# A two-layer encoder on TensorE: activation tiles laid out chunk by chunk as first part and rest with tokens of one parity together, and the attention branch's output projection in two sums

## The chip, the cores and the metric

The kernel runs on one core of a Trainium2 chip. The time is device microseconds of one execution, and a kernel's time is the median of its runs. The core has a matrix engine (PE, with PEld for its weight loads), a vector engine (DVE), an activation engine (ACT), GpSimd (POOL) and a queue of transfers (SP).

## The reference

One sequence of 256 tokens with 1024 channels goes through two layers; all is float32.

```python
def reference(x, w_in, w_pool, ..., norm_f):
    h = x
    for layer in range(DEPTH):
        h = h + _token_mixer(_rmsnorm(h, norm1[layer]), w_in[layer], ...)
        h = h + _conv_ffn(_rmsnorm(h, norm2[layer]), w_up[layer], ...)
    return _rmsnorm(h, norm_f)
```

`_token_mixer` multiplies the normed tokens with one wide matrix `w_in`. Its columns are: 1024 of a pooling branch (four groups, centred means over 2, 4, 8 and 16 tokens minus the token, then a 256x256 matrix per group and a scale), three times 1536 of queries, keys and values (12 heads of 128 in three groups: all keys within 64 tokens, every 4th, every 16th token; the groups are combined by their softmax denominators into 4 x 128 channels), and two times 1024 of gates. The result is `sigmoid(g_pool) * (pool_out @ w_a) + sigmoid(g_attn) * (attn_out @ w_b)`, multiplied by `w_o`. `_conv_ffn` multiplies by `w_up` (two halves of 2816 columns), puts a width-3 convolution over the tokens and a gelu on the first half, multiplies it with the second and by `w_down`.

## The kernel before

**Two parts.** A float32 operand is kept as two tiles of type fp32r: a first part (`xh`, `wh`), which is the operand cast, and a rest (`xl`, `wl`), which is the operand minus that cast. A product is three passes: first by first, first by rest, rest by first.

**Weights** (class `Weights`). A list of pieces, in the order of use, is written out at lines 235 to 282. A transfer of 1 MB (L117, three buffers) brings two pieces. For each, ACT casts the first part (L177) and DVE subtracts it (L178). `get` takes the next piece and has the split of up to three pieces ahead put into the engines' queues; split pieces have five buffers, and a buffer is free when the matmuls of its old piece are done.

**Activations.** `x2` is a tile `[P, 2, KD, S]`: for each channel of a chunk of 128, the first parts of all eight chunks, then the rests, with the 256 tokens in their order. Tokens live in rows by parity (token 2m + t in row m of half t), because the residual stream `h` is `[P, 2, D]`.

- `to_channels` (L432) transposes normed tokens on PE, 128 at a time, and casts and subtracts into `x2` (L454, L455), writing every second word.
- `proj` (L479) makes 128 output channels for all 256 tokens. Per chunk, L485 multiplies `wh` with 512 moving columns (the first parts and the rests of one chunk, 8 KB apart) into both halves of a PSUM tile, and L486 multiplies `wl` with the 256 first parts into the second half. `add_up` (L490) adds the halves: an ACT copy (L492) and a DVE add (L493).
- `row_mm` (L495) and `v_sum` (L562) have the activations as the stationary operand and 512 columns of weights as the moving one: three passes each, on the tokens of one parity, read as `t::2`, every second word. `residual_mm` (L501) calls `row_mm` for the products that are added to `h`; `v_sum` makes the values and the first four chunks of the MLP.
- `first_values` (L697) makes the first layer's values; its raw tile `[P, KD, 2, P]` keeps tokens of one parity together, and L729 reads them in one run.
- `chunk_mm` (L472) makes the three passes as three matmuls of 256 columns, for the pooling matrices (L475 to L477 into pool_ps) and for `w_b` (the same lines into b_ps, called at L1000).

**Order of a layer.** Values; pooling projections (L796); queries and keys (L946) with the steps of attention (`scores`, `turn`, `weigh`) between them; `w_a` (L971); gates of the pooling branch (L986); then twice four gates (L993) and four chunks of `w_b` (L1000 to L1007); `w_o` with the residual; the MLP, where `up` (L1065) makes one chunk (a projection for each half, convolution, gelu) and after two chunks two rows of `w_down` are added. The order of instructions on each engine is chosen by a scheduler from the program's order, but for the beginning, where it is fixed by hand. PSUM has two pools of four banks, `acc` and `mm`.

**The block of w_b.** Per output chunk: 4 x 3 matmuls into b_ps, a DVE multiply with the gate that reads PSUM (L1002), a DVE add of the pooling branch (L1005), an ACT cast (L1006) and a DVE subtraction (L1007).

Of the kernel before, what the change touches and what calls it, by code (L numbers as in the profile page):

```python
# [10 lines left out]
F32 = mybir.dt.float32  # L11
# [193 lines left out]
def encoder(ctx, tc, x, w_in, w_pool, pool_scale, w_a, w_b, w_o, norm1, norm2, w_up, conv_w,  # L205
# [226 lines left out]
    def to_channels(xh, xl, psum, g):  # L432

        tag = "acc" if psum is acc else "mm"

        def fin(t, r, xn):
            for n in range(4):
                cc = slice(n * 256, (n + 1) * 256)  # L440
                nc.vector.scalar_tensor_tensor(
                    out=xn[:, cc], in0=h[:, t, cc], scalar=r[:, 0:1], in1=g[:, cc],
                    op0=ALU.mult, op1=ALU.mult,
                )
            for n in range(2):
                pt = psum.tile([P, 4, P], F32, tag=tag, name="xt_ps")
                ks = slice(4 * n, 4 * n + 4)
                for k in range(4):
                    c0 = (4 * n + k) * P
                    nc.tensor.transpose(pt[:, k, :], xn[:, c0 : c0 + P], ident)  # L450
                oh = xh[:, ks, :].rearrange("p k (m t) -> p k t m", t=2)[:, :, t, :]
                ol = xl[:, ks, :].rearrange("p k (m t) -> p k t m", t=2)[:, :, t, :]
                last = [
                    nc.scalar.copy(out=oh, in_=pt),  # L454
                    nc.vector.tensor_sub(out=ol, in0=pt, in1=oh.bitcast(F32)),  # L455
                ]
                if n == 0:
                    yield
            if t == 1:
                W.queue_behind(last, 6)  # L460

        return fin
# [9 lines left out]
    def chunk_mm(ps, wh, wl, xh, xl, nk):  # L472

        for k in range(nk):
            nc.tensor.matmul(ps, wh(k), xh[:, k, :], start=(k == 0), stop=False)  # L475
            nc.tensor.matmul(ps, wh(k), xl[:, k, :], start=False, stop=False)  # L476
            nc.tensor.matmul(ps, wl(k), xh[:, k, :], start=False, stop=(k == nk - 1))  # L477

    def proj(x2, nk=8):  # L479


        i, (wh, wl) = W.get()
        ps = mmp.tile([P, 2, S], F32, tag="mm", name="proj_ps")
        for k in range(nk):
            nc.tensor.matmul(ps, wh[:, k, :], x2[:, :, k, :], start=(k == 0), stop=False)  # L485
# [15 lines left out]
    def residual_mm(parts, n, done, hold=4, fill=None):  # L501
# [60 lines left out]
    def v_sum(ps, xh, xl, t, n, piece):  # L562

        _, (wh, wl) = piece
        passes = [(xh, wh, 0), (xh, wl, 0), (xl, wh, 0), (xh, wh, 1), (xh, wl, 1), (xl, wh, 1)]
        for m, (a, w, j) in enumerate(passes):
            nc.tensor.matmul(  # L567
                ps, a[:, 2 * n + j, t::2], w[:, j, :], start=(n + m == 0), stop=(n == 3 and m == 5)
            )

    def channel_tiles():
        x2 = big.tile([P, 2, KD, S], F32R, tag="x", name="x2")
        return x2[:, 0], x2[:, 1], x2
# [123 lines left out]
    def first_values(rs, raw_x, fs, done, pe, keep_values):  # L697

        xuh, xul = raw_x
        xh, xl, x2 = channel_tiles()  # L700
# [5 lines left out]
        for k in range(0, KD, 2):  # L706
            f = fs[k // 4][:, k % 4 : k % 4 + 2]
            for j in range(2):
                nc.vector.scalar_tensor_tensor(
                    out=f[:, j], in0=f[:, j], scalar=gcol[:, k + j : k + j + 1], in1=rows,  # L710
                    op0=ALU.mult, op1=ALU.mult,
                )
            oh, ol = (
                a[:, k : k + 2, :].rearrange("p k (m t) -> p k t m", t=2) for a in (xh, xl)
            )
            nc.scalar.copy(out=oh, in_=f)
            nc.vector.tensor_sub(out=ol, in0=f, in1=oh.bitcast(F32))
# [19 lines left out]
    for l in range(DEPTH):  # L737
# [21 lines left out]
        if l == 0:  # L759
            with tc.manual_schedule():  # L760
                begun = begin_values_of_x()
            x2 = first_values(*begun, keep_values)
            xh, xl = x2[:, 0], x2[:, 1]
        else:
            for g in range(NG):
                held = begun[0] if g == 0 else [W.get() for _ in range(4)]
                for t in range(2):
                    if g + t == 0:
                        ps = begun[1]
                    else:  # L770
                        ps = v_tile()
                        for n in range(4):
                            v_sum(ps, xh, xl, t, n, held[n])
                    keep_values(t, g, ps)
                for i, _ in held:
                    W.free(i)
# [8 lines left out]
        plh = big.tile([P, KD, S], F32R, tag="ybig", name="plh")  # L785
        pll = big.tile([P, KD, S], F32R, tag="xn", name="pll")
        pooled = {}
        for gi in range(3, -1, -1):
# [31 lines left out]
            ph, pl = plh[:, 2 * gi : 2 * gi + 2, :], pll[:, 2 * gi : 2 * gi + 2, :]  # L820
# [3 lines left out]
        def pool_out(poh, pol):  # L824
            for j in range(2):
                i, (wh, wl) = W.get()
                for gg in range(2):
                    ph, pl = pooled[2 * j + gg]
                    for oc in range(2):
                        ps = mmp.tile([P, S], F32, tag="mm", name="pool_ps")  # L830
# [6 lines left out]
                        nc.scalar.activation(poh[:, c, :], ps, AF.Copy, scale=sc)  # L837
                        nc.vector.scalar_tensor_tensor(
                            out=pol[:, c, :], in0=ps, scalar=sc, in1=poh[:, c, :].bitcast(F32),
# [11 lines left out]
        at2 = big.tile([P, 2, HPG, S], F32R, tag="at2", name="at2")  # L851
        ath, atl = at2[:, 0], at2[:, 1]
# [51 lines left out]
        def weigh(hh):  # L904
# [13 lines left out]
            oh = ath[:, hh, :].rearrange("p (m t) -> p t m", t=2)  # L918
            ol = atl[:, hh, :].rearrange("p (m t) -> p t m", t=2)
# [14 lines left out]
        for m, c in enumerate(PAIRS):  # L934
            if m == 1:
                po2 = big.tile([P, 2, KD, S], F32R, tag="m2", name="po2")
                poh, pol = po2[:, 0], po2[:, 1]
                pool_parts = pool_out(poh, pol)
# [51 lines left out]
        m2 = big.tile([P, 2, KD, S], F32R, tag="m2", name="m2")  # L990
        mh, ml = m2[:, 0], m2[:, 1]
        for c4 in range(2):
            ths = [gate(4 * c4 + j) for j in range(4)]  # L993
            for j2 in range(2):
                i, (wh, wl) = W.get()
                for j in range(2):
                    c = 4 * c4 + 2 * j2 + j
                    ps = mmp.tile([P, S], F32, tag="mm", name="b_ps")
                    cc = slice(j * P, (j + 1) * P)
                    chunk_mm(ps, lambda k: wh[:, k, cc], lambda k: wl[:, k, cc], ath, atl, 4)  # L1000
                    m = sm.tile([P, S], F32, tag="u", name="m")
                    nc.vector.scalar_tensor_tensor(  # L1002
                        out=m, in0=ths[2 * j2 + j], scalar=1.0, in1=ps, op0=ALU.add, op1=ALU.mult
                    )
                    nc.vector.tensor_add(out=m, in0=m, in1=pa[:, c, :])  # L1005
                    nc.scalar.copy(out=mh[:, c, :], in_=m)  # L1006
                    nc.vector.tensor_sub(out=ml[:, c, :], in0=m, in1=mh[:, c, :].bitcast(F32))  # L1007
                W.free(i)

        xh, xl, x2 = channel_tiles()  # L1010
        norm = Norm(to_channels(xh, xl, acc, g2))
        entry = []

        def begin_mlp():
# [3 lines left out]
            for n in range(3):  # L1018
                v_sum(ps, xh, xl, 0, n, held[n])
            entry.extend((held, ps))  # L1020
            return lambda: v_sum(ps, xh, xl, 0, 3, held[3])

        run(residual_mm(lambda k: (mh[:, k, :], ml[:, k, :]), KD, norm.add, fill=begin_mlp))
# [6 lines left out]
                big.tile([P, n, S], F32R, tag=f"{tag}{j}", name=f"act{tag}{j}")  # L1030
# [24 lines left out]
        for n in range(4):  # L1055
            v_sum(ps, xh, xl, 1, n, held[n])
# [8 lines left out]
        def up(f):  # L1065
# [16 lines left out]
            g = sm.tile([P, S], F32, tag="p", bufs=3, name="g")  # L1082
            add_up(g, sums)
# [15 lines left out]
            ah, al = (x[n >= HPG][:, n - HPG * (n >= HPG), :] for x in (acth, actl))  # L1099
            nc.scalar.copy(out=ah, in_=y2)  # L1100
            nc.vector.tensor_sub(out=al, in0=y2, in1=ah.bitcast(F32))
# [5 lines left out]
        def begin_values():  # L1107

            ps, held = v_tile(), [W.get() for _ in range(4)]
            for n in range(3):  # L1110
                v_sum(ps, xh, xl, 0, n, held[n])
            begun.extend((held, ps))
            return lambda: v_sum(ps, xh, xl, 0, 3, held[3])
# [11 lines left out]
        if l + 1 < DEPTH:  # L1125
            xh, xl, x2 = channel_tiles()
            late["norm"] = Norm(to_channels(xh, xl, mmp, g1))
# [33 lines left out]
```

## Time and profile before

| | |
|---|---|
| median of 3 runs | 891.43 us (890.87 to 891.78) |
| the profiled execution | 890.68 us |
| its span, first to last instruction | 888.9 us |
| granted TensorE clock | 0.999 |
| DMA | 164.47 MB, mean 185 GB/s |
| projections, L485 and L486 | 40.4% and 20.4% of the chain that ended last |
| row_mm, L497 to L499 | 6.3% each |
| v_sum, L567 | 6.3% |
| w_b, L475 to L477 into b_ps | 0.9% each |

The page gives, engine by engine, the busy time; then the span in 40 slices; then the chain that ended last, followed back from the last instruction to what released it; then groups of equal instructions, as "line engine operation out<-in, shape, xcount | busy us, mean ns of one | idle us before". Matmuls are pipelined: one starts before the one ahead of it has ended, so a group's mean duration is longer than what it adds to the time. The chain and the timeline list starts in microseconds, and from these the step between two matmuls is found.

### The profile page before, as it was taken

What the parts mean: (1) busy time and instruction counts of PE and PEld (TensorE: products, weight loads), DVE (VectorE), ACT (ScalarE), POOL (GpSimd) and SP (SyncE); (2) the same over time, 40 slices, a digit from 0 to 9 for tenths busy, and PEclk for the clock granted to TensorE, in tenths of its full rate; (3) what the DMA queues carried; (4) which work ended last, traced back from release to release, by engine and by line L of the source; (5) the groups of instructions that cost most, each with busy time, mean ns of one, the idle gap of its engine ahead of it and who ended that gap; (6) DMA issues with size and microseconds to landing.
All of it is one profiled execution on the core that took longest, in us unless ns stands there. A gap on an engine that the chain in (4) does not pass through costs nothing.

```text
span 888.9 us, 12895 instructions
## 1 busy us (share of the span) xinstructions
PE 881.2 (99%) x4913; PEld 764.5 (86%) x4913; DVE 671.2 (76%) x1135; ACT 516.0 (58%) x897; POOL 13.7 (2%) x40
## 2 busy tenths in 40 slices
PE   9999999999999999999999999999999999999997
PEld 7889889889888888888888898888898888888886
DVE  7988786767759978777855977766677698777784
ACT  7746454555647756666545564554555476666662
POOL 2000000000000000000000000000000000000000
PEclk9999999999999999999999999999999999999999
DMA  9669744455545465565636555443557346465531
GB/s 335 227 206 302 235 143 142 144 189 189 188 168 190 153 227 190 168 211 189 237 119 211 168 190 189 144 161 125 190 189 264 106 155 231 166 202 187 180 143 48
DMA packets 125791, 164.47 MB, mean 185 GB/s; under 512 B 2996, under 2 KB 106108, under 8 KB 125601
## 3 DMA queue, kind: packets, MB, share of 16 engines
q1 hardware_dynamic: 125712, 163.65, 55.1%
q8 instruction: 38, 0.62, 0.3%
q14 instruction: 25, 0.20, 0.1%
q10 hardware_dynamic: 16, 0.00, 0.0%
HBM read 162.57 MB, written 3.69 MB: 187 GB/s over the span
## 4 chain that ended last, share of the span: by engine, by line
PE 99%; ACT 0%; POOL 0%; DVE 0%; issue 0%; POOLq 0%; ACTq 0%
PE proj_ps L485 40%; PE proj_ps L486 20%; PE v_ps L567 6%; PE res_ps L497 6%; PE res_ps L499 6%; PE res_ps L498 6%; PE v_ps L729 2%; PE v_ps L640 1%; PE b_ps L477 1%; PE b_ps L475 1%; PE b_ps L476 1%; PE pt_ps L893 1%; PE o_ps L914 1%; PE s_ps L864 1%; PE s_ps L859 1%; PE o_ps L910 1%
## 5 line engine op out<-in xcount | busy, mean ns | idle before, releaser
L485 PE MATMUL proj_ps<-x,wh 128*128 128x512 f32 x1408 | 498.4, 398 | 0.0
L178 DVE TENSOR_TENSOR wl<-raw,wh 128x1024 fp32r<-128x1024 f32 x274 | 334.5, 1224 | 131.0 <-ACT wh L177 129.3
L177 ACT CAST wh<-raw 128x1024 fp32r<-128x1024 f32 x274 | 287.2, 1052 | 201.3 <-PE proj_ps L485 144.6
L486 PE MATMUL proj_ps<-x,wl 128*128 128x256 f32 x1408 | 394.3, 280 | 0.0
L485 PEld LDWEIGHTS proj_ps<-x,wh 128*128 128x128 f32 x1408 | 264.4, 188 | 63.3 <-issue 0.7
L486 PEld LDWEIGHTS proj_ps<-x,wl 128*128 128x128 f32 x1408 | 265.7, 189 | 1.0 <-issue 0.2
L497 PE MATMUL res_ps<-wh,actq 128*128 128x512 f32 (+1 forms) x184 | 70.9, 385 | 0.0
L498 PE MATMUL res_ps<-wl,actq 128*128 128x512 f32 (+1 forms) x184 | 70.7, 384 | 0.0
L499 PE MATMUL res_ps<-wh,actk 128*128 128x512 f32 (+1 forms) x184 | 70.7, 384 | 0.0
L485 PE MATMUL proj_ps<-po,wh 128*128 128x512 f32 x128 | 46.2, 402 | 0.0
L497 PEld LDWEIGHTS res_ps<-wh,actq 128*128 128x128 f32 x184 | 35.7, 194 | 6.8
L499 PEld LDWEIGHTS res_ps<-wh,actk 128*128 128x128 f32 x184 | 35.6, 194 | 6.8
L498 PEld LDWEIGHTS res_ps<-wl,actq 128*128 128x128 f32 x184 | 35.7, 194 | 6.1
L486 PE MATMUL proj_ps<-po,wl 128*128 128x256 f32 x128 | 35.8, 279 | 0.0
L1074 ACT ACTIVATE y<-a,prm 128x256 f32<-128x256 f32 x36 | 21.7, 603 | 19.2 <-DVE a L493 19.1
L1091 ACT ACTIVATE y<-y 128x256 f32<-128x256 f32 x44 | 18.4, 417 | 21.3 <-DVE y L1088 21.3
L485 PEld LDWEIGHTS proj_ps<-po,wh 128*128 128x128 f32 x128 | 24.0, 188 | 5.0
L416 ACT ACTIVATE junk<-h 128x512 f32<-128x512 f32 (+1 forms) x20 | 11.0, 549 | 29.3 <-DVE h L414 29.3
L497 PE MATMUL res_ps<-wh,m 128*128 128x512 f32 (+1 forms) x72 | 26.7, 371 | 0.0
L498 PE MATMUL res_ps<-wl,m 128*128 128x512 f32 (+1 forms) x72 | 26.6, 369 | 0.0
L499 PE MATMUL res_ps<-wh,m 128*128 128x512 f32 (+1 forms) x72 | 26.6, 369 | 0.0
L567 PE MATMUL v_ps<-wh,x 128*128 128x512 f32 x80 | 26.1, 397 | 0.0
(208 smaller groups left out, 1146.1 us busy)
## 6 DMA issues: line engine op xcount, KB each, us to landing
raw<-in_w_in_dram SPq DMA_DIRECT2D x58, 1024.0 KB, 5.6
raw<-in_w_up_dram SPq DMA_DIRECT2D x44, 1024.0 KB, 5.6
raw<-in_w_down_dram SPq DMA_DIRECT2D x22, 1024.0 KB, 4.8
raw<-in_w_a_dram SPq DMA_DIRECT2D x8, 1024.0 KB, 4.8
raw<-in_w_o_dram SPq DMA_DIRECT2D x8, 1024.0 KB, 4.9
raw<-in_w_b_dram SPq DMA_DIRECT2D x4, 1024.0 KB
sk<-fd SPq DMA_DIRECT2D x1, 2560.0 KB
raw<-in_w_pool_dram SPq DMA_DIRECT2D x2, 1024.0 KB
```

Source lines behind the costliest of these rows:

```text
L177: lambda: nc.scalar.copy(out=h, in_=src),
L178: lambda: nc.vector.tensor_sub(out=l, in0=src, in1=h.bitcast(F32)),
L416: nc.scalar.activation(junk[:, 0 : cc.stop - cc.start], h[:, t, cc], AF.Square, scale=D**-0.5, accum_out=ss[:, n : n + 1],)
L485: nc.tensor.matmul(ps, wh[:, k, :], x2[:, :, k, :], start=(k == 0), stop=False)
L486: nc.tensor.matmul(ps[:, 1], wl[:, k, :], x2[:, 0, k, :], start=False, stop=(k == nk - 1))
L497: nc.tensor.matmul(ps, ah, wh, start=first, stop=False)
L498: nc.tensor.matmul(ps, ah, wl, start=False, stop=False)
L499: nc.tensor.matmul(ps, al, wh, start=False, stop=last)
L567: nc.tensor.matmul(ps, a[:, 2 * n + j, t::2], w[:, j, :], start=(n + m == 0), stop=(n == 3 and m == 5))
L729: nc.tensor.matmul(ps[t], a[:, k, t, :], w[:, j, :], start=(k + m == 0), stop=(k == KD - 1 and m == 2),)
L1074: nc.scalar.activation(y, a, AF.Identity, bias=b, scale=w1)
L1091: nc.scalar.activation(y2, y2, AF.Tanh, scale=c)
```

## The change

Every tile of activations that PE reads is laid out chunk by chunk. `x2` becomes `[P, KD, 2, 2, P]`: for a chunk the first part and then the rest, each as the 128 even tokens and then the 128 odd ones (`two_parts`). `po2` and `at2` likewise; the first parts and rests that stay in two tiles (plh and pll, m2, the MLP's acts) keep their tokens by parity. So the moving operand of a projection is one run of 512 words, and the stationary operand of `row_mm` and `v_sum` is one run of 128.

PSUM tiles now hold tokens by parity. Where the order of tokens matters (the pooled windows in `u`, the convolution's `a`), `add_up` writes every second word through the view `in_order`; the pooled difference `pd` and the gelu's `y2` are read that way when they are turned back. The copies into `x2` and `at2`, and those out of the projections of queries and keys, which stepped by two words, step by one.

For `w_b`, `chunk_mm` is replaced by `two_sums`, the loop of `proj`: per chunk one matmul of 512 columns and one of 256 into the two halves of b_ps, and then `add_up` (one ACT copy and one DVE add more per tile) before the multiply with the gate. The multiplications are the same ones.

```diff
-    def to_channels(xh, xl, psum, g):
+    def to_channels(x2, psum, g):
...
-                oh = xh[:, ks, :].rearrange("p k (m t) -> p k t m", t=2)[:, :, t, :]
-                ol = xl[:, ks, :].rearrange("p k (m t) -> p k t m", t=2)[:, :, t, :]
+                oh, ol = (x2[:, ks, part, t, :] for part in (0, 1))
...
+    def two_sums(ps, wh, wl, x2, nk):
+        for k in range(nk):
+            nc.tensor.matmul(ps, wh(k), x2[:, k], start=(k == 0), stop=False)
+            nc.tensor.matmul(ps[:, 1], wl(k), x2[:, k, 0], start=False, stop=(k == nk - 1))
...
-        for k in range(nk):
-            nc.tensor.matmul(ps, wh[:, k, :], x2[:, :, k, :], start=(k == 0), stop=False)
-            nc.tensor.matmul(ps[:, 1], wl[:, k, :], x2[:, 0, k, :], start=False, stop=(k == nk - 1))
+        two_sums(ps, lambda k: wh[:, k, :], lambda k: wl[:, k, :], x2, KD)
...
+    def halves(a):
+        return a.rearrange("p (t m) -> p t m", t=2)
+
+    def in_order(a):
+        return a.rearrange("p (m t) -> p t m", t=2)
...
-            row_mm(ps_, ah[:, t::2], al[:, t::2], wh[:, 0, cc], wl[:, 0, cc], start, stop)
+            row_mm(ps_, ah[:, t], al[:, t], wh[:, 0, cc], wl[:, 0, cc], start, stop)
...
-                ps, a[:, 2 * n + j, t::2], w[:, j, :], start=(n + m == 0), stop=(n == 3 and m == 5)
+                ps, x2[:, 2 * n + j, part, t, :], w[:, j, :], start=(n + m == 0),
+                stop=(n == 3 and m == 5),
...
+    def two_parts(tag, name):
+        return big.tile([P, KD, 2, 2, P], F32R, tag=tag, name=name)
...
-                add_up(u[:, j, PAD : PAD + S], proj(x2))
+                add_up(in_order(u[:, j, PAD : PAD + S]), [halves(a) for a in proj(x2)])
...
-                src, rest = (s.rearrange("p (m t) -> p t m", t=2) for s in proj(x2))
+                src, rest = (halves(a) for a in proj(x2))
...
-                    ps = mmp.tile([P, S], F32, tag="mm", name="b_ps")
+                    ps = mmp.tile([P, 2, S], F32, tag="mm", name="b_ps")
...
-                    chunk_mm(ps, lambda k: wh[:, k, cc], lambda k: wl[:, k, cc], ath, atl, 4)
+                    two_sums(ps, lambda k: wh[:, k, cc], lambda k: wl[:, k, cc], at2, 4)
                     m = sm.tile([P, S], F32, tag="u", name="m")
+                    add_up(m, (ps[:, 0], ps[:, 1]))
                     nc.vector.scalar_tensor_tensor(
-                        out=m, in0=ths[2 * j2 + j], scalar=1.0, in1=ps, op0=ALU.add, op1=ALU.mult
+                        out=m, in0=ths[2 * j2 + j], scalar=1.0, in1=m, op0=ALU.add, op1=ALU.mult
                     )
...
-                add_up(a, proj(x2))
+                add_up(in_order(a), [halves(b) for b in proj(x2)])
...
             nc.vector.scalar_tensor_tensor(
-                out=y2, in0=y2, scalar=0.5, in1=g, op0=ALU.mult, op1=ALU.mult
+                out=g, in0=in_order(y2), scalar=0.5, in1=g, op0=ALU.mult, op1=ALU.mult
             )
...
-            nc.scalar.copy(out=ah, in_=y2)
-            nc.vector.tensor_sub(out=al, in0=y2, in1=ah.bitcast(F32))
+            nc.scalar.copy(out=ah, in_=g)
+            nc.vector.tensor_sub(out=al, in0=g, in1=ah.bitcast(F32))
```

More of the change, by code (lines that the diff above doesn't have):

```diff
@@ L474, in chunk_mm, with proj @@
         for k in range(nk):
[L475 to L479, printed above, removed]
+            nc.tensor.matmul(ps, wh(k), xh[:, k], start=(k == 0), stop=False)
+            nc.tensor.matmul(ps, wh(k), xl[:, k], start=False, stop=False)
+            nc.tensor.matmul(ps, wl(k), xh[:, k], start=False, stop=(k == nk - 1))
+    def two_sums(ps, wh, wl, x2, nk):
+        for k in range(nk):
+            nc.tensor.matmul(ps, wh(k), x2[:, k], start=(k == 0), stop=False)
+            nc.tensor.matmul(ps[:, 1], wl(k), x2[:, k, 0], start=False, stop=(k == nk - 1))
+    def proj(x2):
         i, (wh, wl) = W.get()
         ps = mmp.tile([P, 2, S], F32, tag="mm", name="proj_ps")
-        for k in range(nk):
-            nc.tensor.matmul(ps, wh[:, k, :], x2[:, :, k, :], start=(k == 0), stop=False)
-            nc.tensor.matmul(ps[:, 1], wl[:, k, :], x2[:, 0, k, :], start=False, stop=(k == nk - 1))
+        two_sums(ps, lambda k: wh[:, k, :], lambda k: wl[:, k, :], x2, KD)
         W.free(i)
         return ps[:, 0], ps[:, 1]
+    def halves(a):
+        return a.rearrange("p (t m) -> p t m", t=2)
+    def in_order(a):
+        return a.rearrange("p (m t) -> p t m", t=2)
     def add_up(out, sums):
@@ L560, in v_tile, with v_sum @@
         return acc.tile([P, 512], F32, tag="acc", name="v_ps")
-    def v_sum(ps, xh, xl, t, n, piece):
+    def v_sum(ps, x2, t, n, piece):
         _, (wh, wl) = piece
-        passes = [(xh, wh, 0), (xh, wl, 0), (xl, wh, 0), (xh, wh, 1), (xh, wl, 1), (xl, wh, 1)]
-        for m, (a, w, j) in enumerate(passes):
+        passes = [(0, wh, 0), (0, wl, 0), (1, wh, 0), (0, wh, 1), (0, wl, 1), (1, wh, 1)]
+        for m, (part, w, j) in enumerate(passes):
             nc.tensor.matmul(
-                ps, a[:, 2 * n + j, t::2], w[:, j, :], start=(n + m == 0), stop=(n == 3 and m == 5)
-            )
-    def channel_tiles():
-        x2 = big.tile([P, 2, KD, S], F32R, tag="x", name="x2")
-        return x2[:, 0], x2[:, 1], x2
+                ps, x2[:, 2 * n + j, part, t, :], w[:, j, :], start=(n + m == 0),
+                stop=(n == 3 and m == 5),
+            )
+    def two_parts(tag, name):
+        return big.tile([P, KD, 2, 2, P], F32R, tag=tag, name=name)
     def begin_values_of_x():
@@ L712, in first_values @@
                 )
-            oh, ol = (
-                a[:, k : k + 2, :].rearrange("p k (m t) -> p k t m", t=2) for a in (xh, xl)
-            )
+            oh, ol = (x2[:, k : k + 2, part] for part in (0, 1))
             nc.scalar.copy(out=oh, in_=f)
@@ L772, in encoder @@
                         for n in range(4):
-                            v_sum(ps, xh, xl, t, n, held[n])
+                            v_sum(ps, x2, t, n, held[n])
                     keep_values(t, g, ps)
@@ L782, in encoder @@
         g2 = gain(norm2[l])
-        plh = big.tile([P, KD, S], F32R, tag="ybig", name="plh")
-        pll = big.tile([P, KD, S], F32R, tag="xn", name="pll")
+        plh = big.tile([P, KD, 2, P], F32R, tag="ybig", name="plh")
+        pll = big.tile([P, KD, 2, P], F32R, tag="xn", name="pll")
         pooled = {}
@@ L829, in pool_out @@
                     for oc in range(2):
-                        ps = mmp.tile([P, S], F32, tag="mm", name="pool_ps")
+                        ps = mmp.tile([P, 2, P], F32, tag="mm", name="pool_ps")
                         cc = slice(oc * P, (oc + 1) * P)
@@ L850, in encoder @@
         kk = big.tile([P, NH - HPG, 2, P], F32, tag="k1", name="k")
-        at2 = big.tile([P, 2, HPG, S], F32R, tag="at2", name="at2")
-        ath, atl = at2[:, 0], at2[:, 1]
+        at2 = big.tile([P, HPG, 2, 2, P], F32R, tag="at2", name="at2")
         probs, ptiles = {}, {}
@@ L917, in weigh @@
                     )
-            oh = ath[:, hh, :].rearrange("p (m t) -> p t m", t=2)
-            ol = atl[:, hh, :].rearrange("p (m t) -> p t m", t=2)
+            oh, ol = at2[:, hh, 0], at2[:, hh, 1]
             nc.scalar.copy(out=oh, in_=ps)
@@ L935, in encoder @@
             if m == 1:
-                po2 = big.tile([P, 2, KD, S], F32R, tag="m2", name="po2")
-                poh, pol = po2[:, 0], po2[:, 1]
-                pool_parts = pool_out(poh, pol)
+                po2 = two_parts("m2", "po2")
+                pool_parts = pool_out(po2)
             if m == 2:
@@ L989, in encoder @@
             )
-        m2 = big.tile([P, 2, KD, S], F32R, tag="m2", name="m2")
+        m2 = big.tile([P, 2, KD, 2, P], F32R, tag="m2", name="m2")
         mh, ml = m2[:, 0], m2[:, 1]
@@ L997, in encoder @@
                     c = 4 * c4 + 2 * j2 + j
-                    ps = mmp.tile([P, S], F32, tag="mm", name="b_ps")
+                    ps = mmp.tile([P, 2, S], F32, tag="mm", name="b_ps")
                     cc = slice(j * P, (j + 1) * P)
-                    chunk_mm(ps, lambda k: wh[:, k, cc], lambda k: wl[:, k, cc], ath, atl, 4)
+                    two_sums(ps, lambda k: wh[:, k, cc], lambda k: wl[:, k, cc], at2, 4)
                     m = sm.tile([P, S], F32, tag="u", name="m")
+                    add_up(m, (ps[:, 0], ps[:, 1]))
                     nc.vector.scalar_tensor_tensor(
-                        out=m, in0=ths[2 * j2 + j], scalar=1.0, in1=ps, op0=ALU.add, op1=ALU.mult
+                        out=m, in0=ths[2 * j2 + j], scalar=1.0, in1=m, op0=ALU.add, op1=ALU.mult
                     )
                     nc.vector.tensor_add(out=m, in0=m, in1=pa[:, c, :])
-                    nc.scalar.copy(out=mh[:, c, :], in_=m)
-                    nc.vector.tensor_sub(out=ml[:, c, :], in0=m, in1=mh[:, c, :].bitcast(F32))
+                    m = halves(m)
+                    nc.scalar.copy(out=mh[:, c], in_=m)
+                    nc.vector.tensor_sub(out=ml[:, c], in0=m, in1=mh[:, c].bitcast(F32))
                 W.free(i)
-        xh, xl, x2 = channel_tiles()
-        norm = Norm(to_channels(xh, xl, acc, g2))
+        x2 = two_parts("x", "x2")
+        norm = Norm(to_channels(x2, acc, g2))
         entry = []
@@ L1018, in begin_mlp @@
             for n in range(3):
-                v_sum(ps, xh, xl, 0, n, held[n])
+                v_sum(ps, x2, 0, n, held[n])
             entry.extend((held, ps))
-            return lambda: v_sum(ps, xh, xl, 0, 3, held[3])
-        run(residual_mm(lambda k: (mh[:, k, :], ml[:, k, :]), KD, norm.add, fill=begin_mlp))
+            return lambda: v_sum(ps, x2, 0, 3, held[3])
+        run(residual_mm(lambda k: (mh[:, k], ml[:, k]), KD, norm.add, fill=begin_mlp))
         g1 = gain(norm1[l + 1] if l + 1 < DEPTH else norm_f)
@@ L1029, in encoder @@
             [
-                big.tile([P, n, S], F32R, tag=f"{tag}{j}", name=f"act{tag}{j}")
+                big.tile([P, n, 2, P], F32R, tag=f"{tag}{j}", name=f"act{tag}{j}")
                 for j, n in enumerate((HPG, NH - HPG))
@@ L1055, in encoder @@
         for n in range(4):
-            v_sum(ps, xh, xl, 1, n, held[n])
+            v_sum(ps, x2, 1, n, held[n])
             if n == 1:
@@ L1081, in up @@
             )
-            g = sm.tile([P, S], F32, tag="p", bufs=3, name="g")
-            add_up(g, sums)
+            g = sm.tile([P, 2, P], F32, tag="p", bufs=3, name="g")
+            add_up(g, [halves(a) for a in sums])
             c = float(np.sqrt(2.0 / np.pi))
@@ L1110, in begin_values @@
             for n in range(3):
-                v_sum(ps, xh, xl, 0, n, held[n])
+                v_sum(ps, x2, 0, n, held[n])
             begun.extend((held, ps))
-            return lambda: v_sum(ps, xh, xl, 0, 3, held[3])
+            return lambda: v_sum(ps, x2, 0, 3, held[3])
         down = residual_mm(
@@ L1125, in encoder @@
         if l + 1 < DEPTH:
-            xh, xl, x2 = channel_tiles()
-            late["norm"] = Norm(to_channels(xh, xl, mmp, g1))
+            x2 = two_parts("x", "x2")
+            late["norm"] = Norm(to_channels(x2, mmp, g1))
         else:
```

14 lines of the change are left out of this document (7 added, 7 removed).

## The prediction

> **What bounds the kernel now.** I read section 1 of the page, then the chain that ended last, then the groups by shape, then the chain and the timeline in short stretches. TensorE (PE) is busy 99% of the span and is 99% of the chain; in the groups its idle time comes to 1.2 us.
>
> ```profile
> PE 881.2 (99%) x4913; PEld 764.5 (86%) x4913; DVE 671.2 (76%) x1135; ACT 516.0 (58%) x897; POOL 13.7 (2%) x40
> PE 99%; ACT 0%; POOL 0%; DVE 0%; issue 0%; POOLq 0%; ACTq 0%
> ```
>
> So the time is the number of matmuls times the step from one start to the next. The "mean ns" of the groups overlap each other (398 and 280 for a pair that starts again after about 350), so I take steps from starts. First the chain, which merges equal neighbours:
>
> ```profile
> 19.96 21.78 PE v_ps L729 x96
> ...
> 132.76 0.70 PE o_ps L910 x6
> ...
> 452.93 28.00 PE v_ps L567 x120
> ```
>
> L729 and L567 do the same work: three passes, 512 moving columns in one run, 128 stationary columns. L729 reads its stationary tile in one run (tokens of a parity together, `a[:, k, t, :]`) and steps by 21.78/96 = 226.9 ns; L567 reads every second word (`t::2`) and steps by 28.00/120 = 233.3 ns. Their weight loads differ too (ns min/median/max):
>
> ```profile
> L729 PEld LDWEIGHTS v_ps<-wh,xuh x32: 187/188/189, 19.7 to 40.7; 128*128 128x128 f32 x32
> ...
> L567 PEld LDWEIGHTS v_ps<-wh,x x80: 193/193/198, 262.5 to 707.0; 128*128 128x128 f32 x80
> ```
>
> Now the projection, a pair of one 512-column matmul (L485, moving operand in two runs of 256) and one of 256 (L486). From the timeline, two stretches:
>
> ```profile
> 58.35 0.39 PE L485 MATMUL proj_ps<-x,wh 128*128 128x512 f32 x1
> ...
> 72.22 0.39 PE L485 MATMUL proj_ps<-x,wh 128*128 128x512 f32 x1
> ...
> 276.60 0.40 PE L485 MATMUL proj_ps<-x,wh 128*128 128x512 f32 x1
> ...
> 302.04 0.40 PE L485 MATMUL proj_ps<-x,wh 128*128 128x512 f32 x1
> ```
>
> Five projections of 8 pairs lie between the first two: 13.87/40 = 346.8 ns a pair. Nine lie between the last two: 25.44/72 = 353.3 ns. Reading all 192 projections so, 70 hold about 346.5 and 122 about 353.3, each for its whole length and often for many in a row; the mean pair is 350.85 (34 longer first steps left out). Operands, shapes and engines at work are the same in both, so there is a **fast and a slow rhythm**, and what came just before decides which is entered. All steady steps here are whole multiples of 6.67 ns: 226.7, 233.3, 346.7, 353.3, and 120.0 for the 256-column matmuls of b_ps (L475 to L477).
>
> **The change, part by part.**
>
> *1. Stationary operands in one run* (row_mm L497 to L499; v_sum L567). Groups by shape give the 512-column matmuls that read `t::2` now: (168 + 56) x 3 = 672 in row_mm and 240 in L567, 912 in all. Each goes from 233.3 to 226.7 ns if the run is what parts L567 from L729: 912 x 6.67 = **-6.1 us**. The 96 of 256 columns step by about 120 ns like those of b_ps, whose operands are in one run already: nothing. Bounds: 0 (the early stretch of L729 is fast for another reason) and -6.1; I take -6.1, because L729 differs in nothing else that the code shows.
>
> [...]
>
> *2. Moving operand of proj in one run.* 1,536 pairs, mean 350.85. The matmul durations hint that the two runs cost a little: L485 lasts 391 ns even in the fast rhythm (395 median, 403 at worst in the slow one), L729 389. That little decides, I think, which multiple a pair is held to. With one run I expect the fast rhythm throughout: 1,536 x (350.85 - 346.7) = **-6.3 us**. Bounds: the lowest steps of the rows for the two halves, 226.9 and 0.70/6 = 116.7 (L910), give 343.6 a pair and -11.1 us; all in the slow rhythm gives 1,536 x (353.3 - 350.85) = +3.8 us.
>
> *3. The attention projection in two sums.* Per chunk k three 256-column matmuls (360 ns) become one of 512 and one of 256, a pair as in proj: 64 x (360 - 346.7) = **-0.85 us**; in the slow rhythm -0.4. PE executes 64 matmuls and 64 weight loads fewer; no other PE instruction moves, and no DMA or queue entry does.
>
> *4. What ACT and DVE get.* Each of the 16 b_ps tiles gets one ACT copy (0.36 us, L492) and one DVE add (0.42, L493), and the multiply that read PSUM reads SBUF (0.42 as L987). In a block of four tiles DVE had 4.95 of 6.00 us busy (window 212 to 218); with 4 x 0.42 it wants 6.6 in a block of 5.6, and a backlog of about 1 us runs into the next 11 us, where DVE is busy 7.8. Behind the new add on DVE stand weight splits (L178), which PE needs next; behind the new copy on ACT stand the casts ahead of those splits (L177). Matching each split with the first matmul that uses it, those used from 206 to 243 us are done 8.4 to 9.2 us early, which hides this. The other wait is for a bank of PSUM: the first tile of a block is drained by about 215.0, its bank is wanted at 220.4 or not before 217.6, so 2.6 us cover it. I cost this at nothing; without cover it is at most 16 x 0.78 = 12.5 us.
>
> *5. Parity order of the copies.* add_up into u and a, and the reads of pd and y2, now step by two words; those into x2, at2, and out of proj for q and k no longer do. DVE shows no price: L921 reads and writes by twos now at 416 ns, L493 in one run takes 419. ACT pays some 30 ns (L920 394 ns, L492 360): 52 copies, 1.6 us, while the 12 casts of L454 (617 ns against 588 for L748) gain 0.35. ACT is 58% busy. DVE is close to its limit in the first part of the MLP (21.78 of 22.00 us in 285 to 307), but its splits are done at least 5 us before use there, and PE comes sooner by less than 1 us. The tightest split of all, 0.3 us, is used at 79.4 in a stretch that already has the fast rhythm. So: nothing; no stall goes, so nothing is late next except at 79.4, by some tenths at most.
>
> **Sum.** -6.1 - 6.3 - 0.85 = -13.2 us. The profiled execution took 890.68 us (span 888.9 and 1.8 around it), so 877.5; the median of the runs shown is 0.75 higher, 891.43. Forecast **878 us**.
>
> **Rivals.**
> - *Rhythm stays.* The projections keep their mixture because the order of the matmuls sets it, not the runs. For: the fast rhythm exists now with two runs. Against: no one-run stream of 512 (L729) is ever seen in a slower steady step. -6.1 - 0.85 (or 0.4): 884.5.
> - *Rhythm yes, stationary no.* What slows L567 and row_mm is also a rhythm, entered for another reason. -6.3 - 0.85: 884.3.
> [...]
> - *A faster rhythm still.* The pair falls to the lower bound of term 2: -6.1 - 11.1 - 1.1: 873.
> - *The slow rhythm everywhere* (the other side). One 512 and one 256 in single runs lock at 353.3, and the stationary operands bring nothing. Place: the 70 projections that are fast now, +3.8 us, with term 3 at -0.4: 894.8. It is slower than before as soon as more than about 8 of those 70 turn slow and neither term 1 nor 2 pays. For: 122 of 192 are slow now, so it is the commoner one. Against: as for the first rival.
>
> **How the numbers follow.** Forecast 0.53; rhythm stays 0.19; stationary no 0.07; layout nothing 0.09; faster still 0.07; slow everywhere 0.05. The predicted time is the forecast's. The range 872 to 886.5 holds the forecast with its splinters, the first two rivals and the faster one (part of the projections may change, and term 4 may cost a microsecond or two); layout nothing and slow everywhere stay outside (0.14), with some more for the unpriced. A measurement of this kernel can tell about 0.2% (1.8 us) from no change: faster 0.86 (the forecast and the rivals at 873 to 884.5), same 0.09 (890.5), slower 0.05.
>
> **What would show it.** Right, step by step: v_ps of the second layer, 120 in a row, in 27.2 us rather than 28.00, and weight loads of row_mm and v_sum at 188 ns, not 193 (term 1); every projection's pairs at 346.7 and no stretch at 353.3 (term 2); b_ps in 16 groups of four such pairs (term 3); PE idle time still about 1 us and no wait for DVE or ACT in it (terms 4 and 5). Wrong: projections still in stretches at 353.3; row_mm still at 233.3 with loads of 188; PE waiting for wl (L178) or for the new copy behind b_ps; DVE adds into a or u well above 0.42 us.

## The result, and the profile after

The changed kernel takes **885.22 us** (median of 6 runs, 884.95 to 885.99) against 891.09 us for the kernel before (6 runs): the ratio is 0.9933, 95% interval 0.9923 to 0.9944. It is faster by 5.9 us where 13.2 were forecast. The profiled execution spans 883.5 us, 5.4 less than before.

The page after, its engines and its chain:

```profile
PE 875.9 (99%) x4849; PEld 755.9 (86%) x4849; DVE 676.8 (77%) x1151; ACT 520.2 (59%) x913; POOL 13.1 (1%) x40
...
PE 99%; ACT 0%; POOL 0%; DVE 0%; issue 0%; POOLq 0%; ACTq 0%
```

PE is still the whole chain, with 64 matmuls fewer. Who waited on PE (us in total, times, longest):

```profile
PE gain_ps L333 <- DVE ones L319: 1.0, 1, 1.0
PE v_ps L653 <- ACT xuh L609: 0.2, 1, 0.2
```

That is the 1.2 us of the start, as before: nothing that the change adds makes PE wait. So the gain is in the steps. In the chain, v_sum is now L578 (L740 is the first layer's loop that already read in one run):

```profile
20.16 21.78 PE v_ps L740 x96
...
450.65 27.23 PE v_ps L578 x120
```

27.23/120 = 226.9 ns, where it was 233.3: exactly the step of L740. The weight loads of row_mm (L497 before, L508 now) and v_sum came down with it (ns min/median/max); the first line is of the kernel before:

```profile
L497 PEld LDWEIGHTS res_ps<-wh,actq x184: 193/193/198, 304.8 to 881.9; 128*128 128x128 f32 x184
...
L508 PEld LDWEIGHTS res_ps<-wh,actq x184: 187/188/192, 303.6 to 876.5; 128*128 128x128 f32 x184
...
L578 PEld LDWEIGHTS v_ps<-wh,x x80: 187/188/190, 261.5 to 702.8; 128*128 128x128 f32 x80
```

The projections, from the timeline; the first two lines are three gates (24 pairs) apart, the last two nine projections of the MLP (72 pairs):

```profile
217.63 0.39 PE L482 MATMUL proj_ps<-x,wh 128*128 128x512 f32 x1
...
225.95 0.39 PE L482 MATMUL proj_ps<-x,wh 128*128 128x512 f32 x1
...
275.49 0.40 PE L482 MATMUL proj_ps<-x,wh 128*128 128x512 f32 x1
...
300.93 0.40 PE L482 MATMUL proj_ps<-x,wh 128*128 128x512 f32 x1
```

8.32/24 = 346.7 ns and 25.44/72 = 353.3 ns: **both rhythms are still there**, with the moving operand in one run. Of 192 projections 64 are fast and 128 slow, 17 of these behind one short first pair of 340 ns; the mean pair is 350.91 against 350.85. From the starts in the trace, the slow rhythm isn't a steady step either: pairs of about 361, 349 and 350 ns repeat, in both kernels, and 353.3 is their mean. In the projections of the pooling stage shown in the prediction every pair takes 346 or 347 ns.

Summing the steps from start to start of all PE instructions by the tile that they write shows where the time went, here with three kernels of the experiments (us):

| | before | changed | e1 | e9 | e12 |
|---|---|---|---|---|---|
| proj_ps | 542.4 | 542.5 | 539.2 | 538.4 | 538.6 |
| res_ps (row_mm) | 168.4 | 164.9 | 164.4 | 164.2 | 168.2 |
| v_ps | 90.8 | 89.7 | 89.7 | 90.0 | 91.2 |
| b_ps | 23.0 | 22.2 | 22.5 | 22.3 | 23.0 |
| span | 888.9 | 883.5 | 880.2 | 879.0 | 884.9 |

### The profile page after: what moved, and what is told of

Same layout as the page of the kernel before. It is cut to its first block, busy times and chain, and to the rows that moved or that the text cites. A ratio compares the mean times of both kernels' runs of the same rounds, so it can differ in the third digit from the quotient of the medians.

```text
span 883.5 us, 12773 instructions
## 1 busy us (share of the span) xinstructions
PE 875.9 (99%) x4849; PEld 755.9 (86%) x4849; DVE 676.8 (77%) x1151; ACT 520.2 (59%) x913; POOL 13.1 (1%) x40
## 4 chain that ended last, share of the span: by engine, by line
PE 99%; ACT 0%; POOL 0%; DVE 0%; issue 0%; POOLq 0%; ACTq 0%
PE proj_ps L482 41%; PE proj_ps L483 20%; PE res_ps L508 6%; PE res_ps L510 6%; PE v_ps L578 6%; PE res_ps L509 6%; PE v_ps L740 2%; PE b_ps L482 2%; PE v_ps L653 1%; PE pt_ps L903 1%; PE b_ps L483 1%; PE o_ps L924 1%; PE s_ps L874 1%; PE s_ps L869 1%; PE o_ps L920 1%; PE xt_ps L450 1%
## 5 line engine op out<-in xcount | busy, mean ns | idle before, releaser
L483 PE MATMUL proj_ps<-x,wl 128*128 128x256 f32 x1408 | 394.1, 280 | 0.0
L483 PEld LDWEIGHTS proj_ps<-x,wl 128*128 128x128 f32 x1408 | 265.6, 189 | 0.9 <-issue 0.2
L508 PE MATMUL res_ps<-wh,actq 128*128 128x512 f32 (+1 forms) x184 | 70.5, 383 | 0.0
L508 PEld LDWEIGHTS res_ps<-wh,actq 128*128 128x128 f32 x184 | 34.6, 188 | 6.9
L483 PE MATMUL proj_ps<-po,wl 128*128 128x256 f32 x128 | 35.7, 279 | 0.0
L508 PE MATMUL res_ps<-wh,m 128*128 128x512 f32 (+1 forms) x72 | 26.5, 368 | 0.0
L578 PE MATMUL v_ps<-wh,x 128*128 128x512 f32 x80 | 25.7, 392 | 0.0
```

What stands on the lines that cost most here:

```text
L483: nc.tensor.matmul(ps[:, 1], wl(k), x2[:, k, 0], start=False, stop=(k == nk - 1))
L508: nc.tensor.matmul(ps, ah, wh, start=first, stop=False)
L578: nc.tensor.matmul(ps, x2[:, 2 * n + j, part, t, :], w[:, j, :], start=(n + m == 0), stop=(n == 3 and m == 5),)
```

## The experiments

**Theory A**: a projection alternates two widths, and strict alternation has two stable rhythms; what came before picks one, and no layout of the projection's operands ends it. **Rival L**: the runs of an operand set the step (what the prediction held). **Rival N**: the traffic of the other engines in a stage does.

### e1: wide, then narrow

```diff
-        for k in range(nk):
-            nc.tensor.matmul(ps, wh(k), x2[:, k], start=(k == 0), stop=False)
-            nc.tensor.matmul(ps[:, 1], wl(k), x2[:, k, 0], start=False, stop=(k == nk - 1))
+        for k0 in range(0, nk, 8):
+            for k in range(k0, min(k0 + 8, nk)):
+                nc.tensor.matmul(ps, wh(k), x2[:, k], start=(k == 0), stop=False)
+            for k in range(k0, min(k0 + 8, nk)):
+                nc.tensor.matmul(ps[:, 1], wl(k), x2[:, k, 0], start=False, stop=(k == nk - 1))
```

With 8 chunks (4 in w_b, which runs through the same loop) all wide matmuls of a tile come first, then all narrow ones.

> The changed kernel (885.2 us) with one edit: in two_sums all matmuls of 512 columns of a projection come first, then all of 256; the same products, only the order of the sum differs. Theory A (the strict alternation of 512 and 256 has two stable rhythms, 346.7 and 353.3 ns a pair, and what came before picks one): without alternation there is one step for each, 8 x 226.7 + 8 x 120 = 2773 ns a projection against a mean of 8 x 350.9 = 2807, less some settling at each change of width: 4 to 6 us faster, 879 to 881. Rival N (the traffic of the other engines in a stage slows the matmuls there): the same stages stay slow, 885, within 1 us.

Measured 881.91 us (0.9896, 0.9881 to 0.991). The chain now merges the equal neighbours; here in the pooling stage, which was fast, and in the MLP, which was slow (L483 wide, L485 narrow):

```profile
64.26 1.84 PE proj_ps L483 x8
66.10 0.95 PE proj_ps L485 x8
67.05 1.84 PE proj_ps L483 x8
...
281.30 1.84 PE proj_ps L483 x8
283.14 0.95 PE proj_ps L485 x8
284.09 1.84 PE proj_ps L483 x8
```

A projection takes 2.79 us in both stages; the alternation took 8 x 346.7 = 2.77 in the one and 8 x 353.3 = 2.83 in the other. This is as theory A has it, and N falls: the neighbours in time are the same, only the order is another. Short of the 4 to 6 us expected, it gains 3.3: after each change of width the first five wide steps are 233, 236, 228, 233, 231 ns.

### e2: the same order with the old layout

The order of e1 in the projections of the kernel before (one line is added, a second `for k in range(nk):`); the moving operand stays in two runs 8 KB apart, and w_b keeps its three passes.

> The kernel before (891.1 us), moving operand of the projection still in two runs 8 KB apart, with wide then narrow. Theory A, with the runs worth nothing: the wide steps are 226.7 and it gains what e1 gains, 885 to 887. Rival L (what the prediction held: the second run costs something that shows in a stream): wide steps of 233.3 throughout, 8 x 233.3 + 8 x 120 = 2826 ns a projection, 1,536 x 2.4 ns = 3.8 us slower, 895.

Measured 888.16 us (ratio to before 0.9964, 0.9951 to 0.9977). Its chain in the MLP (L485 wide, L487 narrow):

```profile
281.29 0.95 PE proj_ps L487 x8
282.25 1.84 PE proj_ps L485 x8
284.08 0.95 PE proj_ps L487 x8
285.04 1.84 PE proj_ps L485 x8
```

The same 1.84 and 0.95 us: two runs cost the moving operand nothing. Rival L is refuted for proj. Its projections take 539.3 us, those of e1 539.2; it gains the 3 us that e1 gained, and misses the 885 to 887 expected by the settling that e1 showed.

### e3: the stationary operand of row_mm alone

```diff
-            row_mm(ps_, ah[:, t::2], al[:, t::2], wh[:, 0, cc], wl[:, 0, cc], start, stop)
+            row_mm(ps_, ah[:, t], al[:, t], wh[:, 0, cc], wl[:, 0, cc], start, stop)
```

and m2 and the acts `[.., 2, P]`, in the kernel before.

> The kernel before (891.1 us) with only the stationary operands of row_mm (m2 and the MLP's acts) laid out by parity; x2, the projections, v_sum and w_b as they were. If the run of the stationary operand is the cause: 672 matmuls from 233.3 towards 226.7, as in the changed kernel some 3.5 us (4.5 without settling): 887 to 887.6, and v_sum still at 233.3. If the step of row_mm is a rhythm set by something else: 891 within 1 us.

Measured 888.22 us (0.9965, 0.9952 to 0.9978), 3.1 us faster; row_mm takes 164.9 us as in the changed kernel. Its weight loads:

```profile
L498 PEld LDWEIGHTS res_ps<-wl,actq x184: 187/188/192, 304.8 to 879.4; 128*128 128x128 f32 x184
```

And v_sum, untouched, in the chain:

```profile
451.78 28.00 PE v_ps L567 x120
```

So for the stationary operand it is the run that counts (L holds there), in the same kernel in which v_sum, still read by twos, stays at 233.3. Its projections, which it does not touch, take 543.0 us where the kernel before had 542.4; e8 comes back to this.

### e4: w_b in three passes again

The changed kernel with `chunk_mm(.., at2[:, :, 0], at2[:, :, 1], 4)` for w_b and no add_up.

> The changed kernel (885.2 us) with w_b again as three matmuls of 256 columns and no add_up there. Its own price: 64 x (360 - 346.7) = 0.85 us slower, 886.1. Theory A says more: after matmuls of 256 alone the four gates behind the block fall back into the slow rhythm that they had before, 2 x 4 x 8 x 6.7 ns = 0.4 us, so 886.4; the next engines' work there is lighter, so N would make the gates no slower, 886.1 or below.

Measured 886.54 us; b_ps 23.0 us (+0.8) and the projections 542.9 (+0.35). Gates behind the block start at 217.60 and, three projections on, at 226.08: 8.48/24 = 353 ns where the changed kernel had 346.7. A change in one stage altered the rhythm of the next, which it does not touch. In all it is 1.3 us slower, as theory A reckoned; the medians alone are too close to tell (ratio to before 0.9949, 0.9932 to 0.9965, against 0.9933, 0.9923 to 0.9944), so it is the steps that show it.

### e5 and e9: another order in every second projection, and two by two

e5 runs, in every second projection, one wide, all narrow, then the other wide matmuls; the other projections are as in e1. e9 replaces the loop of the changed kernel by

```diff
+        for k0 in range(0, nk, 2):
+            for k in range(k0, min(k0 + 2, nk)):
+                nc.tensor.matmul(ps, wh(k), x2[:, k], start=(k == 0), stop=False)
+            for k in range(k0, min(k0 + 2, nk)):
+                nc.tensor.matmul(ps[:, 1], wl(k), x2[:, k, 0], start=False, stop=(k == nk - 1))
```

> The changed kernel with wide then narrow as in e1 (881.9 us), but every second projection runs one wide matmul (which opens the sum), all narrow ones, then the other wide ones, so that neighbours meet at the same width. In e1 each run of wide matmuls after narrow ones starts 233, 236, 228, 233, 231 ns before it settles at 226.7, about 28 ns over, and each run of narrow ones starts some 8 ns under 120: 20 ns a change of width there and back. Theory A (a change of width costs a settling): half of 192 such changes go, 1.9 us faster than e1, 880.0. If the settling belongs to the beginning of a projection (its new PSUM tile or its new weights), nothing changes: 881.9.

> The changed kernel with the projection in the order wide, wide, narrow, narrow. Theory A in its simplest form, from the settling seen in e1 (233, 236, then 113, 119): 701 ns for two pairs, 350.5 a pair everywhere, so about as the changed kernel, 884 to 885.5, and no stretches of two kinds any more. If this order too has a fast rhythm that it locks into: 346.7 in some stretches, 881 to 884.

Measured 880.82 us for e5 (0.9887, 0.987 to 0.9903), 1.1 below e1. Its expectation had miscounted: the one wide matmul that opens the sum stands between narrow ones, so two projections still have four changes of width, as in e1 (within and between neighbouring projections the trace has 370, e1 326). Their steps fall by only 0.3 us, and that says nothing of the price of a change. What does is row_mm: in e5 all 16 that follow a projection come behind a wide matmul, start at 226 or 227 ns at once, where e1's begin with 234, 236, 228, 232 and 231, and res_ps as a whole takes 0.5 us less. The projections that come behind a wide matmul start at 226 or 227 as well. The settling belongs to the change of width, then, and not to the beginning of a projection.

Measured **880.33 us** for e9 (0.988, 0.9866 to 0.9895), the fastest of these kernels. Its chain:

```profile
281.37 0.46 PE proj_ps L483 x2
281.84 0.23 PE proj_ps L485 x2
282.07 0.47 PE proj_ps L483 x2
282.54 0.23 PE proj_ps L485 x2
282.76 0.46 PE proj_ps L483 x2
283.23 0.23 PE proj_ps L485 x2
283.46 0.47 PE proj_ps L483 x2
```

Two pairs take (283.46 - 281.37)/3 = 0.697 us, 348.3 ns a pair, and 155 of the 192 projections take 2,776 to 2,787 ns (most of the others begin with a longer first step): one rhythm everywhere. Neither expectation had it: it is not 350.5, and not the fast one either.

### e6, e10, e11: another entry

One matmul of 128 columns, one of 256, or two of 256, overwritten at once, ahead of the first projection behind each row_mm of the MLP.

> The changed kernel (885.2 us) with one more matmul, of 128 columns and overwritten at once, ahead of the first projection after each block of row_mm in the MLP (7 in each layer, 14 in all). Its own price: 14 x 108 ns = 1.5 us. Theory A (what comes before picks the rhythm): the 56 projections behind them, which all run at 353 now, go to 346.7 in part or whole, down to -3.0 us, so 883.7 to 886.7 and other rhythms in those stretches of the trace. Rival N (the traffic of the stage sets it): they stay at 353, 886.7.

> As the kernel with one matmul of 128 columns ahead of the projections behind row_mm (887.1 us), but with 256 columns, so another phase at the entry. Its own price: 14 x 120 ns = 1.7 us over the changed kernel's 885.2. If the entry picks the rhythm: with 56 projections at 346.7 instead of 353.3, -3.0 us, 883.9; if these stretches can't leave the slow rhythm: 886.9.

> The same with two matmuls of 256 columns ahead (a third phase). Price: 14 x 240 ns = 3.4 us over 885.2. Entry picks the rhythm and hits the fast one: 885.6; stays slow: 888.6.

Measured 887.07, 886.83 and 888.51 us, each close to the changed kernel plus the price of the extra matmuls (886.7, 886.9 and 888.6). The rhythm behind them is the slow one in all three; the only difference is that the short first pair of 340 ns is gone. Three phases missed: these edits did not steer the entry, and N would have said the same.

### e8: every fourth word

```diff
-                big.tile([P, n, S], F32R, tag=f"{tag}{j}", name=f"act{tag}{j}")
+                big.tile([P, n // 2, S, 2], F32R, tag=f"{tag}{j}", name=f"act{tag}{j}")
...
```

> The kernel before (891.1 us) with the MLP's acts of two chunks interleaved word by word, so that the stationary operand of their row_mm (504 matmuls of 512 columns) is every fourth word instead of every second; ACT and DVE write them by twos. If a break of the run costs one step of 6.67 ns whatever its width: 233.3 as before, 891. If it is the number of pieces of memory that a weight load touches: two steps, 240, and loads longer than 193 ns, 504 x 6.67 = 3.4 us slower, 894.5. [...]

Measured 897.53 us (1.0071, 1.0056 to 1.0086). Weight loads of the acts, and of m2, which stayed every second word:

```profile
L498 PEld LDWEIGHTS res_ps<-wl,actq x184: 308/309/338, 305.9 to 888.7; 128*128 128x128 f32 x184
L498 PEld LDWEIGHTS res_ps<-wl,m x72: 193/193/197, 235.6 to 698.3; 128*128 128x128 f32 x72
```

In these runs a load took longer the further apart its words lay: 188 ns for every word (e3), 193 for every second, 309 for every fourth. Behind 512 columns the settled step grows little, to 235.0 (231, 240, 231, 238 repeat) from 233.3, not to the 240 expected. The mean is 238.7 only because each of the 16 row_mm begins with a step of some 350 ns. The 256-column matmuls, which lost nothing by twos (median 120 ns before and after), go from 121.5 to 230.3, which the expectation had left out, and bring most of the loss (48 x 109 ns = 5.2 us); 0.9 us more are two waits of PE, for DVE and ACT, that the kernel before does not have. So most of what it is slower by is not the step that was forecast. For every second word against every word the runs gave 5 ns a load (193 against 188) and 6.7 ns a step (233.3 against 226.7).

The surprise is behind it. The projections of the MLP are those of the kernel before, line for line. Here three of them in the timeline of e8:

```profile
328.43 0.40 PE L485 MATMUL proj_ps<-x,wh 128*128 128x512 f32 x1
...
336.76 0.39 PE L485 MATMUL proj_ps<-x,wh 128*128 128x512 f32 x1
```

And the same three in the timeline of the kernel before:

```profile
327.17 0.39 PE L485 MATMUL proj_ps<-x,wh 128*128 128x512 f32 x1
...
335.64 0.40 PE L485 MATMUL proj_ps<-x,wh 128*128 128x512 f32 x1
```

8.33/24 = 347 ns against 8.47/24 = 353 ns. All 56 projections behind a row_mm of the MLP are fast, where only 8 were in the kernel before, with their own layout and order unchanged: what came before does pick the rhythm, though e6, e10 and e11 failed to.

The traces show more of it than the edits tried. In the kernel before, the two row_mm with fast projections behind them end unsettled (230, 237, 229, 236 ns), and the other twelve end at about 233, with slow ones behind them. In e8 all fourteen end unsettled (232, 238, 230, 231). In the changed kernel and in e3 all fourteen end at 226 or 227, and all 56 projections are slow: the layout of row_mm, which made row_mm faster, took the fast rhythm from 8 projections (0.4 us). In these kernels and in e4, every steady stream of row_mm, v_sum or w_b (226.7, 233.3 or 120 ns) right ahead of the alternation is followed by the slow rhythm. No experiment made that condition alone, so it is a regularity and not a shown cause; and unsteady is not enough, since in the kernel before the projections behind a v_sum that ends 235, 238, 233, 229 are slow.

### e12 and e13: the order alone, and the order by stage

e12 is the order of e9 in the kernel before; e13 is e9 with the plain alternation in the pooling projections, w_a, gates and w_b.

> The kernel before (891.1 us), with its old layout, and only the order wide, wide, narrow, narrow in the projections. If the runs of the moving operand are worth nothing in this order too: 2787 ns a projection as in the changed kernel with this order, which took 4.1 us off its projections: 887.0, and row_mm and v_sum still at 233.3. If the two runs cost something once the rhythm is out of the way: more than 2787 ns, above 887.5. What is left to the changed kernel with this order (880.3) is then the layout's own worth with the order held: 6.7 us.

> The changed kernel with wide, wide, narrow, narrow in queries, keys and the MLP, and the plain alternation where it was fast already (pooling projections, w_a, gates, w_b): there 2773 ns a projection rather than 2787, if the fast rhythm is still entered behind the other order. About 50 projections x 14 ns = 0.7 us: 879.6 against 880.3. If they are entered in the slow rhythm, up to 50 x 39 ns = 2 us slower, 882.3.

Measured 887.21 us for e12 (0.9956, 0.994 to 0.9973): 538.6 us of projections with the old layout, 538.4 in e9 with the new. The whole change (layout and w_b) with this order held is worth 887.21 - 880.33 = 6.9 us by the medians, 5.9 by the spans of the two profiled executions (884.9 and 879.0). Measured 880.82 us for e13, no gain: the gates of both layers took 2,773 ns, but the second layer's eight pooling projections 2,809 to 2,831. These stand behind a v_sum and were slow in the changed kernel too; the expectation had counted them as fast.

## Why the prediction was right or wrong

- *What bounds it*: right. PE waits 1.2 us as before, and every microsecond is found in steps.
- *1, stationary operands*: right in mechanism (e3 for row_mm; for v_sum the loads and steps before and after), 233.3 to 226.9 in a settled stream. The size was 4.6 us (3.5 in row_mm, 1.1 in the v_ps tiles), not 6.1: behind a projection the first ten steps of a row_mm are 241, 237, 233, 236, 224, 231, 236, 228, 233 and 231 ns, some 60 ns over, and the settled step had been multiplied by all 912. The term also left out what it does to the stage behind: 8 projections turned slow with it (e3, e8).
- *2, moving operand*: **this step failed.** "With one run I expect the fast rhythm throughout" put -6.3 us on the layout; it measured +0.1. The hint it rested on, 391 ns of duration against 389, was no evidence: e2 and e12 give the same steps with two runs and with one. The rhythm is a matter of order (e1, e9) and of what comes before (e4, e8); what at the entry decides stays open. Nor is a slow pair held to a multiple of 6.67 ns: 353.3 is only the mean of three unequal pairs. (The product is -6.4, not -6.3.) The prediction had written that the fast rhythm exists with two runs, and then did not draw the conclusion.
- *3, w_b*: right, -0.8 us in b_ps, and 0.35 more that no step had, because the gates behind it turned fast (e4). Elsewhere projections turned slow, those 8 of the MLP and some of queries and keys, and that the sum over all projections came out even is chance.
- *4, ACT and DVE*: right. In the window of the first block and in the 11 us behind it:

```profile
211.50:217.00 5.50, 5.50 (x34) 4.80 (x33) 4.17 (x8) 3.91 (x8) 0.00 (x0) 1.00 0.57 194
217.00:228.00 11.00, 11.00 (x65) 9.61 (x65) 9.93 (x20) 7.22 (x14) 0.00 (x0) 1.00 0.57 191
```

DVE (the third busy column) isn't full in the block itself, as the forecast had it, but carries more into the second window, 9.93 us there instead of 7.8, and PE does not notice. The cover shrank: the split used at 247.4 us is done 0.9 us ahead, where the same one had 2.6.

- *5, parity order*: right. The DVE adds into `a`, which write and read by twos, take the same 418 ns as those into `g`, in one run:

```profile
L504 DVE TENSOR_TENSOR g<-proj_ps,g 128x256 f32<-128x256 f32 x44 | 18.4, 418 | 0.8 <-ACT g L503 0.8
L504 DVE TENSOR_TENSOR a<-proj_ps,a 128x256 f32<-128x256 f32 x36 | 15.1, 418 | 0.0
```

ACT pays 378 ns for `a` where it was 359, and 386 for `u` where it was 366.

- *The rivals*: "rhythm stays" is what happened, forecast at 884.5 and given 0.19, with term 1 still at -6.1. Its reason, that the order and not the runs sets the mixture, is what e1, e2 and e9 show; that the stage ahead has its part (e4, e8) it did not say. "Layout nothing", 890.5 with a chance of 0.09, is the sum with term 3 alone; e3 measured 3.1 us for the stationary operand of row_mm in one run.

## What to carry to other kernels

Where PE is the whole chain, take the settled step from start to start of each kind of matmul, and look whether one and the same code shows two of them in different stretches; if it does, try the order of widths: here it brought about 4 us (e12) and cost nothing. The stationary operand in one run was worth 3.1 us here (e3); the moving one could stay in two (539.3 us of projections in e2, 539.2 in e1). A small difference in a mean duration (391 ns against 389) was no cause here: a gain that rests on one should first be tried alone, as e2 does with one line.

## What the runs showed of the hardware that was not expected

- Two settled rhythms of one alternation of 512 and 256 columns, 346.7 and 353.3 ns a pair, each held for many projections (before and changed); the slow one repeats over three pairs (361, 349, 350). Two by two, one rhythm of 348.3 (e9).
- In these runs a stream of 512 columns settled at 226.7 ns after five matmuls behind eight of 256 (e1), after ten behind most alternating projections (row_mm of the changed kernel), and at once behind 512 columns (e5).
- Right behind a steady stream of row_mm, v_sum or w_b the alternation of before, changed, e3, e4 and e8 is slow in every case; behind a row_mm that ends unsettled it is fast (2 in before, 14 in e8).
- The settled streams of these runs stepped by 226.7 (512 columns, stationary in one run: changed, v_sum), 233.3 (every second word: before, v_sum) and 120.0 ns (256: before, w_b): multiples of 6.67 ns; the 235.0 of every fourth word (e8) and the 348.3 of two by two (e9) are not. What sets that unit, and which condition at the entry picks a rhythm, stays open; e6, e10 and e11 found no way to steer it, and e8 did so unintended.
